# Expert routing of a two-block transformer on one NeuronCore: GpSimd's part of the look-up moved to VectorE in float16, one-hots by token pairs, expert tiles placed between the routing's parts

## The chip, the cores and the metric

The kernel runs on one core of a Trainium2 chip. The metric is the device time of one execution in microseconds (us), lower is better. The engines are named as the profile names them: PE is TensorE's matmul, PEld its weight load, DVE is VectorE, ACT is ScalarE, POOL is GpSimd, SP is SyncE, which here only issues DMAs.

## What is computed

The program is two transformer blocks over 512 tokens of width 1024 in float32. The change lies in the first block's expert layer (PEER): every token picks, in each of 8 heads, 16 of 16,384 experts by a product of two key tables of 128 keys each.

```python
def chunk(xc):                                   # 128 tokens at a time
    q = (xc @ peer_wq).reshape(TOKEN_CHUNK, PEER_HEADS, PEER_DQ)
    s1 = jnp.einsum('chd,nd->chn', q[..., :half], peer_keys[0])
    s2 = jnp.einsum('chd,nd->chn', q[..., half:], peer_keys[1])
    v1, i1 = lax.top_k(s1, PEER_TOPK)            # 16 best of 128 keys
    v2, i2 = lax.top_k(s2, PEER_TOPK)
    cand_s = (v1[..., :, None] + v2[..., None, :]).reshape(TOKEN_CHUNK, PEER_HEADS, -1)
    cand_i = (i1[..., :, None] * N_KEYS + i2[..., None, :]).reshape(TOKEN_CHUNK, PEER_HEADS, -1)
    top_s, pos = lax.top_k(cand_s, PEER_TOPK)    # 16 best of 256 pairs
    e = jnp.take_along_axis(cand_i, pos, axis=-1)
    g = jax.nn.softmax(top_s, axis=-1)
    h = jax.nn.gelu(jnp.einsum('cd,chkd->chk', xc, peer_u[e]))
    return jnp.einsum('chk,chkd->cd', g * h, peer_v[e])
```

## The kernel before

A scheduler orders each engine's instructions ahead of time from the order of the program and from its own estimate of when each can start. The order on every engine is then fixed; an instruction waits in its engine's queue until its inputs and its buffer are there, and everything behind it waits too.

The expert layer is `peer` (from L558). Three of the four blocks of 128 tokens (ND = 3, 384 tokens) are done densely: for each of the 128 expert tiles of 128 experts, TensorE computes all the products of tokens and experts, and a weight table of tokens by experts, zero where a token did not pick an expert, multiplies them. The fourth block is done by gathering the picked rows with indirect DMAs that GpSimd issues (L777 to L796). The stages are these.

1. Queries and first top-16. 16 query tiles of `peer_wq` are multiplied (L635), scored against the keys (L640), and VectorE picks 16 of 128 by its 8-wide maximum, its index search and its replacing of found values (L646 to L650).
2. Routing, the loop over the token blocks `order` = 0, 1, 3, 2 (L682 to L770). GpSimd copies the key indices to float32 (`fi`, L684) and adds the two lists to 256 sums per head (`cand`, L690); VectorE picks 16 of 256 (L696 to L700). The key index behind each pick is looked up with a one-hot over 16 places: VectorE compares (`oh`, L723, float32, four heads at a time), GpSimd multiplies by the indices (L725), VectorE adds up (`e`, L726).
3. Weight table. For the three dense blocks, VectorE makes one-hots over the 128 keys for 8 tokens at a time in float16, `o1` and `o2` (L758), and `og`, which is `o1` times the gate's high and low part (L761). The tokens lie in groups of four beside each other (`iota4`, `by4`). For each token TensorE multiplies the one-hots with a contraction over the picks (L766), ScalarE copies four tokens' results to `wb` (L768), and a DMA stores 32 tokens' table in HBM (`w_d`, L770). There are 48 such steps of 8 tokens, 96 instructions each of `o` and `og`, and 768 matmuls of 128 columns.
4. Ahead tiles. 68 of the 128 expert tiles (NA) have no need of the routing for their product of tokens and experts; `ahead` (L654) computes it (24 matmuls of 384 columns, L264 to L266), applies the gelu (L610) and stores it (`gh_d`, L656). In the program these calls stand after the routing (L822, L826); the scheduler places them on TensorE between the routing's matmuls.
5. Main loop over 32 groups of four expert tiles (L831 to L846): weights loaded from the table (L800, two buffers `wt`), `up` for the next group (L803), the split of a value tile into a high part and a rest (`v_split`, L668, two buffers each, one tile ahead), and 18 matmuls of 512 columns per tile (L844).

The expert tiles come through the class `Stream` (L221): SP loads a tile of 128x1024 (L235), ScalarE rounds it to TensorE's short float format (`wh`, L245), and GpSimd subtracts to get the rest (`wl`, L247). With `dve=0` no subtraction of this stream goes to VectorE. Raw tile, high part and rest share a pool of 12 buffers.

Of the kernel before, what the change touches and what calls it, by code (L numbers as in the profile page):

```python
# [9 lines left out]
F32R = mybir.dt.float32r  # L10
# [8 lines left out]
P = 128  # L19
# [201 lines left out]
class Stream:  # L221


    def __init__(self, c, srcs, raw=3, ahead=1, pool=None, dve=0):
        self.pool, self.dve = pool, dve
        self.c, self.srcs, self.rawn, self.ahead = c, srcs, raw, ahead
        self.raw, self.split = {}, {}
        self.i = self.nl = self.ns = 0
        self.limit = len(srcs)
# [9 lines left out]
    def do_split(self, n):  # L239
        c = self.c  # L240
        while self.ns < min(n, self.limit):
            self.load(self.ns + 1)
            r = self.raw.pop(self.ns)
            h, lo = c.t4("wh", F32R, pool=self.pool), c.t4("wl", F32R, pool=self.pool)
            c.nc.scalar.copy(h, r)  # L245
            eng = c.nc.vector if self.dve and self.ns % self.dve == 0 else c.nc.gpsimd
            eng.tensor_sub(lo, r, h)  # L247
            self.split[self.ns] = (h, lo)
            self.ns += 1
            self.load(self.ns + self.rawn - 1)  # L250
# [307 lines left out]
def peer(c, st, st_u, last):  # L558
# [56 lines left out]
    iota16 = iota[:, 0:16]  # L615

    iota4 = c.sm("iota4", [P, P, 4], F16, bufs=1)
    nc.vector.tensor_copy(iota4, iota[:, :, None].to_broadcast([P, P, 4]))
# [39 lines left out]

    esB = Pools(c)
# [8 lines left out]
    def v_split(et):  # L668

        if et >= NE:  # L670
            return
        r = vraw.pop(et)
        h, lo = (vp.tile([P, D], F32R, name=f"v{n}{et}", tag=f"v{n}", bufs=2) for n in "hl")
        for e in range(2):
            s = slice(e * 512, (e + 1) * 512)
            nc.scalar.copy(h[:, s], r[:, s])  # L676
            (nc.vector if e % 2 else nc.gpsimd).tensor_sub(lo[:, s], r[:, s], h[:, s])  # L677
        vsplit[et] = (h, lo)
        v_load(et + VRAW)


    for i in order:  # L682
        fi = se("fi", [P, 8, 2, 16], bufs=2)
        nc.gpsimd.tensor_copy(fi, ti[i])  # L684
        ts = se("ts", [P, 8, 16], bufs=2)
        px = se("px", [P, 8, 16], U32, bufs=2)
        for h4 in range(2):
            hs = slice(h4 * 4, h4 * 4 + 4)
            cand = c.t4("cand", pool=c.c4x).rearrange("p (h a b) -> p h a b", h=4, a=16)
            nc.gpsimd.tensor_tensor(cand, tv[i][:, hs, 0, :, None].to_broadcast([P, 4, 16, 16]),  # L690
# [20 lines left out]
        for half in range(2):  # L711
            pu = se("pu", [P, 8, 16], U32, bufs=2)
            if half == 0:
                nc.vector.tensor_scalar(pu, px, 4, None, op0=OP.logical_shift_right)
            else:
                nc.vector.tensor_scalar(pu, px, 15, None, op0=OP.bitwise_and)
            pf = se("pf", [P, 8, 16], bufs=2)
            nc.vector.tensor_copy(pf, pu)
            e = se("e", [P, 8, 16], bufs=4)
            for h4 in range(2):  # L720
                hs = slice(h4 * 4, h4 * 4 + 4)
                oh = c.t4("oh", pool=c.c4x).rearrange("p (h a b) -> p h a b", h=4, a=16)
                nc.vector.tensor_tensor(oh, pf[:, hs, :, None].to_broadcast([P, 4, 16, 16]),  # L723
                                        iota16[:, None, None, :].to_broadcast([P, 4, 16, 16]), op=OP.is_equal)
                nc.gpsimd.tensor_tensor(oh, oh, fi[:, hs, half, None, :].to_broadcast([P, 4, 16, 16]), op=OP.mult)  # L725
                nc.vector.tensor_reduce(e[:, hs, :], oh, axis=AX.X, op=OP.add)  # L726
            idx.append(e.rearrange("p h k -> p (h k)"))
# [10 lines left out]
        if i == order[-1]:  # L738
            esE.close()
            vp = esB.open("c8", 2)  # L740
            for et in range(VRAW):
                v_load(et)
            v_split(0)
# [6 lines left out]
        shape = [P, TG // 4, P, 4]  # L750
        by4 = lambda a: a.rearrange("p (q t) -> p q t", t=4)[:, :, None, :].to_broadcast(shape)
        for b in range(P // TB):
            wb = c.sm("wb", [P, NE, TB], bufs=2)
            for h in range(TB // TG):
                ts = slice(b * TB + h * TG, b * TB + (h + 1) * TG)
                o1, o2 = c.sm("o1", shape, F16, bufs=1), c.sm("o2", shape, F16, bufs=3)
                for o, a in ((o1, 0), (o2, 1)):
                    nc.vector.tensor_tensor(o, iota4[:, None, :, :].to_broadcast(shape), by4(sl[:, a, ts]), op=OP.is_equal)  # L758
                og = [c.sm("og", shape, F16, bufs=5) for _ in range(2)]
                for n in range(2):  # L760
                    nc.vector.tensor_mul(og[n], o1, by4(gs[:, n, ts]))  # L761
# [36 lines left out]
    def weights(gi):  # L798
        wt = c.sm("wt", [P, GE * SD], bufs=2).rearrange("p (b e t) -> p b e t", b=SD // TB, e=GE)
# [1202 lines left out]
def build(tc, ins, outs, at, phases=(1, 2, 3)):  # L2002
    nc = tc.nc
    with ExitStack() as es:
# [23 lines left out]
        if n1 + n2:  # L2028
# [13 lines left out]
            if 2 in phases:  # L2042
                peer(c, st, Stream(c, [ins["uT"][k] for k in pre_tiles()]), last)
# [32 lines left out]
```

## Time and profile before

| What | Value |
|---|---|
| median of 3 runs | 3082.31 us (3079.56 to 3094.72) |
| the profiled execution's own time | 3063.27 us |
| its span | 3061.3 us |
| mean granted clock of TensorE | 0.957 |
| PE / PEld / DVE / ACT / POOL busy | 93% / 80% / 75% / 39% / 59% |
| stretch of stages 2 to 4 in the profile | about 411 to 853 us |
| stretch of stage 5 | about 853 to 1655 us |

The durations that the profile gives come from the one profiled execution. Busy time counts the time from the start to the end of an instruction; successive instructions of one engine overlap a little, so the time from start to start is shorter than the duration. [...] For an idle time the profile names the instruction whose end released it.

### The profile page before, as it was taken

The page shows a single profiled execution, that of the slowest core. Times are in us where ns is not written, and L with a number is a line of the kernel's source. Part 1 is how long each engine was busy: PE and PEld are TensorE (multiplying, and loading weights), DVE is VectorE, ACT ScalarE, POOL GpSimd, SP SyncE. Part 2 cuts the span into 40 slices and gives each one's busy share as a digit, 9 for nine tenths or more (in the row PEclk, how much of TensorE's full clock was granted, in tenths as well). Part 3 has the DMA queues.
Part 4 walks back from the last instruction along what each step waited for, and adds up shares of the span by engine and source line. Part 5 has one row for each costly group of instructions (what it writes and reads, how often), then busy time and mean ns, then how long its engine had stood idle before and what let it go on. Part 6 is the DMA issues. An engine that isn't in the chain of part 4 may idle for free. (4 is left out here: it accounts for less than half of the span.)

```text
span 3061.3 us, 42565 instructions
## 1 busy us (share of the span) xinstructions
PE 2855.0 (93%) x15507; PEld 2433.8 (80%) x15507; DVE 2309.1 (75%) x3734; ACT 1208.4 (39%) x2077; POOL 1806.8 (59%) x1231
## 2 busy tenths in 40 slices
PE   6789997889999999999999899899999998999998
PEld 5557897779978888888887677688887877888887
DVE  7985899997188999999998688968345874477721
ACT  4444334456333333333334432211225764444431
POOL 5544465543667888888885376623347754554444
PEclk9789998999999999999999999998999999999999
DMA  3101244446799999999996555453753226322232
GB/s 131 41 14 57 77 129 127 173 156 249 237 338 316 327 335 335 323 324 341 332 336 212 177 161 165 139 172 104 222 159 99 76 70 214 120 90 93 93 96 76
DMA packets 270918, 554.01 MB, mean 181 GB/s; under 512 B 41394, under 2 KB 147890, under 8 KB 268916
## 3 DMA queue, kind: packets, MB, share of 16 engines
q1 hardware_dynamic: 219264, 370.91, 37.8%
q0 software_dynamic: 36864, 134.23, 12.0%
q10 hardware_dynamic: 14580, 46.15, 4.2%
q8 instruction: 122, 2.00, 0.3%
q14 instruction: 88, 0.72, 0.1%
HBM read 464.77 MB, written 83.89 MB: 179 GB/s over the span
## 5 line engine op out<-in xcount | busy, mean ns | idle before, releaser
L247 POOL TENSOR_TENSOR wl<-wr,wh 128x1024 fp32r<-128x1024 f32 x319 | 812.9, 2550 | 557.8 <-ACT wh L245 297.9
L245 ACT CAST wh<-wr 128x1024 fp32r<-128x1024 f32 x319 | 334.7, 1050 | 611.5 <-PE mm L265 201.3
L788 DVE CUSTOM_DVE_ANT_0 ur<-ur,hnt 128x1024 f32<-128x1024 f32 x128 | 216.8, 1695 | 74.2 <-DMA ur<-in_u,eix 72.9
L779 POOL DMA_INDIRECT ur<-in_u,eix x128 | 169.5, 1324 | 63.7 <-DVE hc L788 34.4
L677 POOL TENSOR_TENSOR vl<-vr,vh 128x512 fp32r<-128x512 f32 x128 | 190.9, 1492 | 23.6 <-ACT vh L676 18.1
L677 DVE TENSOR_TENSOR vl<-vr,vh 128x512 fp32r<-128x512 f32 x128 | 183.4, 1433 | 25.8 <-issue 16.8
L796 DVE SCALAR_TENSOR_TENSOR acc<-vr,hc,acc 128x1024 f32<-128x1024 f32 x128 | 193.5, 1512 | 1.8 <-DMA vr<-in_vrow,eix 1.7
L779 POOL DMA_INDIRECT vr<-in_vrow,eix x128 | 155.5, 1215 | 47.1 <-issue 24.0
L676 ACT CAST vh<-vr 128x512 fp32r<-128x512 f32 x256 | 145.6, 619 | 76.2 <-issue 31.1
L844 PE MATMUL pb<-vl,ah 128*128 128x512 f32 x512 | 168.9, 397 | 0.0
L844 PE MATMUL pb<-vh,al 128*128 128x512 f32 x512 | 166.4, 395 | 0.0
L844 PE MATMUL pb<-vh,ah 128*128 128x512 f32 x512 | 163.1, 399 | 2.4 <-ACT ah L817 2.4
L766 PE MATMUL pb<-og,o 128*128 128x128 f16 x768 | 105.8, 296 | 41.6 <-DVE og L761 41.2
L766 PEld LDWEIGHTS <-o 128*128 128x128 f16 x768 | 82.7, 119 | 59.6 <-DVE og L761 28.5
L768 ACT ACTIVATE wb<-pb 128x512 f32<-128x512 f32 x96 | 98.9, 1139 | 71.6 <-PE pb L766 71.1
L353 DVE SCALAR_TENSOR_TENSOR acc<-hp,vecs,acc 128x512 f32<-128x512 f32 x100 | 115.8, 1173 | 0.7
L844 PEld LDWEIGHTS pb<-vh,ah 128*128 128x128 f32 x512 | 97.3, 190 | 23.7 <-ACT ah L817 2.7
L844 PEld LDWEIGHTS pb<-vl,ah 128*128 128x128 f32 x512 | 97.2, 190 | 23.0
L844 PEld LDWEIGHTS pb<-vh,al 128*128 128x128 f32 x512 | 97.2, 190 | 22.9
L758 DVE TENSOR_TENSOR o<-iota,sl 128x1024 f16<-128x1024 f16 x96 | 105.4, 1126 | 11.1 <-ACT sl L737 6.9
L1927 POOL TENSOR_TENSOR prob<-prob,nz 128x128 f32<-128x128 f32 (+3 forms) x128 | 88.6, 724 | 39.4 <-DVE nz L1924 27.6
L1152 DVE TENSOR_TENSOR tot<-tot,sq 128x512 f32<-128x512 f32 x11 | 17.0, 1548 | 112.9 <-ACT sq L1149 112.9
(1404 smaller groups left out, 8991.0 us busy)
## 6 DMA issues: line engine op xcount, KB each, us to landing
wr<-in_ws SPq DMA_DIRECT2D x191, 512.0 KB
wr<-in_uT SPq DMA_DIRECT2D x128, 512.0 KB
vr<-in_vrow SPq DMA_DIRECT2D x128, 512.0 KB
w_d<-wb ACTq DMA_DIRECT2D x12, 2048.0 KB
wt<-w_d SPq DMA_DIRECT2D x32, 768.0 KB
gh_d<-gh ACTq DMA_DIRECT2D x68, 192.0 KB
gh<-gh_d SPq DMA_DIRECT2D x68, 192.0 KB
rd_d<-z SPq DMA_DIRECT2D x24, 256.0 KB
```

The costliest lines, as they stand in the source:

```text
L245: c.nc.scalar.copy(h, r)
L247: eng.tensor_sub(lo, r, h)
L353: nc.vector.scalar_tensor_tensor(acc[j], hp[:, tap:tap + S], w[:, tap:tap + 1], acc[j], op0=OP.mult, op1=OP.add)
L676: nc.scalar.copy(h[:, s], r[:, s])
L677: (nc.vector if e % 2 else nc.gpsimd).tensor_sub(lo[:, s], r[:, s], h[:, s])
L758: nc.vector.tensor_tensor(o, iota4[:, None, :, :].to_broadcast(shape), by4(sl[:, a, ts]), op=OP.is_equal)
L766: nc.tensor.matmul(wp[:, u * P:(u + 1) * P], o2[:, q, :, u], og[n][:, q, :, u], start=n == 0, stop=n == 1)
L768: nc.scalar.activation(wb[:, :, t4:t4 + 4].rearrange("p e t -> p t e"), wp.rearrange("p (t e) -> p t e", t=4), AF.Copy, scale=1.0 / GSCALE)
L779: nc.gpsimd.indirect_dma_start(out=t, out_offset=None, in_=src, in_offset=bass.IndirectOffsetOnAxis(ap=eix[:, s:s + 1], axis=0))
L788: nc.vector.tensor_tensor_reduce(out=u, in0=u, in1=hnt, scale=1.0, scalar=0.0, op0=OP.mult, op1=OP.add, accum_out=hc[:, s:s + 1])
L796: nc.vector.scalar_tensor_tensor(acc, v, ghs[gi][:, s:s + 1], acc, op0=OP.mult, op1=OP.add)
L844: nc.tensor.matmul(outs[i][half], ps[a][:, ts], vs[v][:, half * 512:(half + 1) * 512], start=et == 0 and n == 0, stop=et == NE - 1 and n == 2)
```

## The change

Five things are changed.

- The subtractions `wl` of 46 expert tiles (numbers 12 to 57 of this stream) go from GpSimd to VectorE (`dve=range(NTOP, NTOP + NROUTE)`).
- The routing no longer uses GpSimd: `cand` is added on VectorE, `fi` is made there in float16 with each index written twice, and the look-up runs in float16 on 2048 elements at once: one comparison with a table of places, one multiplication, three halving additions and a last one.
- The one-hots over 128 keys are laid out by pairs of tokens (`iota2`, `by2`) where they were by groups of four. The counts and sizes of the instructions stay; TensorE reads every second element where it read every fourth.
- The ahead tiles are called between the routing's parts: 12 ahead of it, 4 at the start of each token block, and one in two of three steps of 8 tokens.
- In the main loop the value tiles are split three ahead (four buffers each of high part and rest) and the weights are loaded two groups ahead (three buffers).

```diff
@@ class Stream
-            eng = c.nc.vector if self.dve and self.ns % self.dve == 0 else c.nc.gpsimd
+            eng = c.nc.vector if self.ns in self.dve else c.nc.gpsimd
             eng.tensor_sub(lo, r, h)
@@ constants
+VAHEAD = 3
 NA = 68
+NTOP = 12
+NSEL = 4
+NROUTE = NT * NSEL + ND * 10
@@ def peer
-    iota4 = c.sm("iota4", [P, P, 4], F16, bufs=1)
+    iota2 = c.sm("iota2", [P, P, 2], F16, bufs=1)
...
+    place = c.sm("place", [P, 16, 16], F16, bufs=1)
+    nc.vector.tensor_copy(place, iota[:, 0:16, None].to_broadcast([P, 16, 16]))
...
+    ahead(NTOP)
...
-        h, lo = (vp.tile([P, D], F32R, name=f"v{n}{et}", tag=f"v{n}", bufs=2) for n in "hl")
+        h, lo = (vp.tile([P, D], F32R, name=f"v{n}{et}", tag=f"v{n}", bufs=VAHEAD + 1) for n in "hl")
...
     for i in order:
-        fi = se("fi", [P, 8, 2, 16], bufs=2)
-        nc.gpsimd.tensor_copy(fi, ti[i])
+        ahead(NSEL)
+
+        fi = se("fi", [P, 2, P, 2], F16, bufs=2)
+        for half in range(2):
+            nc.vector.tensor_copy(fi[:, half].rearrange("p (h a) t -> p h a t", h=8),
+                                  ti[i][:, :, half, :, None].to_broadcast([P, 8, 16, 2]))
...
-            nc.gpsimd.tensor_tensor(cand, tv[i][:, hs, 0, :, None].to_broadcast([P, 4, 16, 16]),
+            nc.vector.tensor_tensor(cand, tv[i][:, hs, 0, :, None].to_broadcast([P, 4, 16, 16]),
...
+            oh = c.t4("oh", F16, 2048, pool=c.c4x)
+            oj = oh.rearrange("p (h j k) -> p h j k", h=8, j=16)
+            nc.vector.tensor_tensor(oj, pf[:, :, None, :].to_broadcast([P, 8, 16, 16]),
+                                    place[:, None, :, :].to_broadcast([P, 8, 16, 16]), op=OP.is_equal)
+            ok = oh.rearrange("p (j k t) -> p j k t", k=8, t=2)
+            nc.vector.tensor_mul(ok, ok, fi[:, half, :, None, :].to_broadcast([P, P, 8, 2]))
+            for n in (8, 4, 2):
+                nc.vector.tensor_add(oj[:, :, 0:n, :], oj[:, :, 0:n, :], oj[:, :, n:2 * n, :])
             e = se("e", [P, 8, 16], bufs=4)
-            for h4 in range(2):
-                hs = slice(h4 * 4, h4 * 4 + 4)
-                oh = c.t4("oh", pool=c.c4x).rearrange("p (h a b) -> p h a b", h=4, a=16)
-                nc.vector.tensor_tensor(oh, pf[:, hs, :, None].to_broadcast([P, 4, 16, 16]),
-                                        iota16[:, None, None, :].to_broadcast([P, 4, 16, 16]), op=OP.is_equal)
-                nc.gpsimd.tensor_tensor(oh, oh, fi[:, hs, half, None, :].to_broadcast([P, 4, 16, 16]), op=OP.mult)
-                nc.vector.tensor_reduce(e[:, hs, :], oh, axis=AX.X, op=OP.add)
+            nc.vector.tensor_add(e, oj[:, :, 0, :], oj[:, :, 1, :])
...
-            v_split(0)
+            for et in range(VAHEAD):
+                v_split(et)
...
-        shape = [P, TG // 4, P, 4]
+        shape = [P, TG // 2, P, 2]
...
             for h in range(TB // TG):
+                if (b * (TB // TG) + h) % 3:
+                    ahead(1)
...
-                            nc.tensor.matmul(wp[:, u * P:(u + 1) * P], o2[:, q, :, u], og[n][:, q, :, u], start=n == 0, stop=n == 1)
+                            nc.tensor.matmul(wp[:, u * P:(u + 1) * P], o2[:, q * 2 + u // 2, :, u % 2],
+                                             og[n][:, q * 2 + u // 2, :, u % 2], start=n == 0, stop=n == 1)
...
-        wt = c.sm("wt", [P, GE * SD], bufs=2).rearrange("p (b e t) -> p b e t", b=SD // TB, e=GE)
+        wt = c.sm("wt", [P, GE * SD], bufs=3).rearrange("p (b e t) -> p b e t", b=SD // TB, e=GE)
...
-            v_split(et + 1)
+            v_split(et + VAHEAD)
@@ def build
-                peer(c, st, Stream(c, [ins["uT"][k] for k in pre_tiles()]), last)
+                peer(c, st, Stream(c, [ins["uT"][k] for k in pre_tiles()], dve=range(NTOP, NTOP + NROUTE)), last)
```

In the changed kernel's line numbers L774 makes the one-hots (L758 before), L777 their products (L761 before), L683 the rests of the value tiles (L677 before), and L661, L785 and L787 are L656, L768 and L770 before. L732, L735, L737 and L739 are the new look-up. The numbers behind the names only tell buffers apart.

The first place is VectorE's queue in the routing, where one token block's look-up meets another block's one-hots. Before:

```order
L758 TENSOR_TENSOR o_746_3762<-iota_534_2466,sl_3639 128x1024
L758 TENSOR_TENSOR o_738_3731<-iota_534_2466,sl_3639 128x1024
L707 RECIPROCAL gz_4153<-gz_4153 128x8
L723 TENSOR_TENSOR oh_4162<-pf_4159,iota_2464 128x1024
L723 TENSOR_TENSOR oh_4166<-pf_4159,iota_2464 128x1024
L723 TENSOR_TENSOR oh_4175<-pf_4172,iota_2464 128x1024
L761 TENSOR_TENSOR og_3735<-o_738_3731,gs_3642 128x1024
L761 TENSOR_TENSOR og_3736<-o_738_3731,gs_3642 128x1024
L708 TENSOR_TENSOR g_4150<-g_4150,gz_4153 128x128
L758 TENSOR_TENSOR o_752_3790<-iota_534_2466,sl_3639 128x1024
L726 TENSOR_REDUCE e_4161<-oh_4162 128x64
```

The same engine and place with the change:

```order
L777 TENSOR_TENSOR og_4638<-o_884_4634,gs_4197 128x1024
L777 TENSOR_TENSOR og_4639<-o_884_4634,gs_4197 128x1024
L247 TENSOR_TENSOR wl_5101<-wr_5036,wh_5100 128x1024
L735 TENSOR_TENSOR oh_6215<-oh_6215,fi_6156 128x2048
L774 TENSOR_TENSOR o_902_4725<-iota_534_2466,sl_4194 128x1024
L735 TENSOR_TENSOR oh_6227<-oh_6227,fi_6156 128x2048
L706 MAX ts_6377<-cand_6379 128x8 x4
L774 TENSOR_TENSOR o_890_4662<-iota_534_2466,sl_4194 128x1024
L247 TENSOR_TENSOR wl_5255<-wr_5070,wh_5254 128x1024
L737 TENSOR_TENSOR oh_6215<-oh_6215 128x8x128
```

The expert tiles' subtractions (L247) now stand in VectorE's queue about every sixth row, and the multiplications of the look-up (L735) too.

The second place is GpSimd's queue in the routing. Before:

```order
L690 TENSOR_TENSOR cand_3580<-tv_2470 128x1024
L684 CAST fi_3554<-ti_2474 128x256
L684 CAST fi_4102<-ti_2475 128x256
L247 TENSOR_TENSOR wl_5489<-wr_5424,wh_5488 128x1024
L247 TENSOR_TENSOR wl_5523<-wr_5458,wh_5522 128x1024
L247 TENSOR_TENSOR wl_5557<-wr_5492,wh_5556 128x1024
L725 TENSOR_TENSOR oh_3614<-oh_3614,fi_3554 128x1024
L725 TENSOR_TENSOR oh_3618<-oh_3618,fi_3554 128x1024
```

With the change:

```order
L247 TENSOR_TENSOR wl_3908<-wr_3843,wh_3907 128x1024
L683 TENSOR_TENSOR vl_6473<-vr_6466,vh_6472 128x512
L683 TENSOR_TENSOR vl_6481<-vr_6468,vh_6480 128x512
L683 TENSOR_TENSOR vl_6489<-vr_6470,vh_6488 128x512
L683 TENSOR_TENSOR vl_7715<-vr_6478,vh_7714 128x512
L247 TENSOR_TENSOR wl_7208<-wr_7057,wh_7207 128x1024
```

The first row is the last expert tile ahead of the routing; the next is the first value tile's split, which belongs to the routing's end. Between them GpSimd has nothing in its queue.

The third place is ScalarE's queue at the last store of the weight table, in which the numbers behind `gh_d` count the ahead tiles from 0 to 67. Before:

```order
L656 DMA gh_d46_2441<-gh_1318_6912 128x384
L768 ACTIVATE wb_1053_5187<-pb_1070_5252 128x4x128
L768 ACTIVATE wb_1053_5187<-pb_1071_5262 128x4x128
L768 ACTIVATE wb_1053_5187<-pb_1076_5280 128x4x128
L768 ACTIVATE wb_1053_5187<-pb_1077_5290 128x4x128
L770 DMA w_d_2463<-wb_1053_5187 128x4096
L245 CAST wh_1340_7052<-wr_1332_6988 128x1024
```

With the change:

```order
L661 DMA gh_d58_2453<-gh_1371_7334 128x384
L785 ACTIVATE wb_1331_7115<-pb_1358_7248 128x4x128
L785 ACTIVATE wb_1331_7115<-pb_1359_7258 128x4x128
L785 ACTIVATE wb_1331_7115<-pb_1364_7276 128x4x128
L785 ACTIVATE wb_1331_7115<-pb_1365_7286 128x4x128
L245 CAST wh_1393_7474<-wr_1385_7410 128x1024
L787 DMA w_d_2463<-wb_1331_7115 128x4096
```

Before, 21 ahead tiles (47 to 67) were left when the table was done; with the change 9 are left (59 to 67).

## Rows read from the trace of the kernel before

**Rows 1.** The page, part 2: busy tenths in 40 slices of 76.5 us.
```profile
PE   6789997889999999999999899899999998999998
...
DVE  7985899997188999999998688968345874477721
...
POOL 5544465543667888888885376623347754554444
```

**Rows 2.** Stretches: from:to, length, PE PEld DVE ACT POOL (instructions), PEclk, DMA share, GB/s.
```profile
411.00:762.00 351.00, 306.80 (x1915) 288.35 (x1914) 329.53 (x550) 179.26 (x213) 196.07 (x77) 0.93 0.50 171
762.00:853.00 91.00, 88.64 (x508) 87.83 (x507) 17.09 (x23) 30.09 (x45) 53.83 (x30) 1.00 0.77 253
853.00:1655.00 802.00, 786.54 (x3703) 679.13 (x3702) 746.82 (x775) 284.56 (x526) 655.69 (x430) 0.99 0.92 325
```

**Rows 3.** Waits from 411 to 762 us: us in all, times, longest us.
```profile
POOL wl L247 <- ACT wh L245: 103.5, 23, 12.5
...
PE pb L766 <- DVE og L761: 41.2, 25, 7.6
PEld L766 <- DVE og L761: 28.5, 19, 7.9
...
ACT wh L245 <- PE po L265: 16.0, 7, 3.3
```

**Rows 4.** Instructions by line, 411 to 762 us: busy us, mean ns, idle before.
```profile
L247 POOL TENSOR_TENSOR wl<-wr,wh 128x1024 fp32r<-128x1024 f32 x48 | 130.1, 2713 | 124.6 <-ACT wh L245 103.5 <-issue 14.4 <-PE po L266 5.8
...
L758 DVE TENSOR_TENSOR o<-iota,sl 128x1024 f16<-128x1024 f16 x96 | 105.4, 1126 | 11.1 <-ACT sl L737 6.9 <-PE pb L766 3.7
...
L761 DVE TENSOR_TENSOR og<-o,gs 128x1024 f16<-128x1024 f16 x96 | 98.9, 1067 | 2.0 <-PE pb L766 1.5
...
L245 ACT CAST wh<-wr 128x1024 fp32r<-128x1024 f32 x47 | 49.5, 1053 | 30.7 <-PE po L265 16.0 <-POOL wl L247 10.8 <-DMA wr<-in_uT 1.9
L725 POOL TENSOR_TENSOR oh<-oh,fi 128x1024 f32<-128x1024 f32 x16 | 47.7, 2996 | 23.2 <-DVE oh L723 23.2
L723 DVE TENSOR_TENSOR oh<-pf,iota 128x1024 f32<-128x1024 f32 x16 | 26.3, 1687 | 0.0
...
L726 DVE TENSOR_REDUCE e<-oh 128x64 f32<-128x1024 f32 x16 | 19.2, 1208 | 2.4 <-POOL oh L725 2.4
```

**Rows 5.** VectorE in order of time: start us, duration us, instruction, count.
```profile
619.45 3.48 DVE L723 TENSOR_TENSOR oh<-pf,iota 128x1024 f32<-128x1024 f32 x3
...
622.96 8.35 DVE L758 TENSOR_TENSOR o<-iota,sl 128x1024 f16<-128x1024 f16 x3
...
657.89 1.89 DVE L758 TENSOR_TENSOR o<-iota,sl 128x1024 f16<-128x1024 f16 x3
```

**Rows 6.** GpSimd in the same stretch.
```profile
625.14 8.36 POOL L725 TENSOR_TENSOR oh<-oh,fi 128x1024 f32<-128x1024 f32 x3
```

**Rows 7.** TensorE in the same stretch; in brackets the idle time before.
```profile
628.54 0.34 PE L265 MATMUL po<-px2l,wh 128*128 128x384 f32 x1
636.46 0.40 PE L766 MATMUL pb<-og,o 128*128 128x128 f16 x2 [7.58 <-DVE og L761]
...
646.00 0.34 PE L264 MATMUL po<-px4h,wh 128*128 128x384 f32 x1
...
649.30 0.34 PE L265 MATMUL po<-px2l,wh 128*128 128x384 f32 x1
```

**Rows 8.** All instances of a line: duration ns least/median/longest, first and last start.
```profile
L758 DVE TENSOR_TENSOR o<-iota,sl x96: 673/685/2897, 453.7 to 754.8; 128x1024 f16<-128x1024 f16 x96
...
L708 DVE TENSOR_TENSOR g<-g,gz x3: 2258/2422/2483, 436.4 to 631.2; 128x128 f32<-128x128 f32 x3
```

**Rows 9.** TensorE's waits in the main loop, 853 to 1655 us.
```profile
PE po L844 <- POOL vl L677: 6.3, 5, 2.3
PE po L844 <- ACT vh L676: 5.3, 2, 2.9
```

**Rows 10.** Stretches again: 50 us in the middle of the main loop.
```profile
1100.00:1150.00 50.00, 50.00 (x241) 43.44 (x240) 48.36 (x50) 18.65 (x34) 41.97 (x29) 1.00 0.94 336
```

More of the change, by code (lines that the diff above doesn't have):

```diff
@@ L221, with __init__ @@
 class Stream:
-    def __init__(self, c, srcs, raw=3, ahead=1, pool=None, dve=0):
+    def __init__(self, c, srcs, raw=3, ahead=1, pool=None, dve=()):
         self.pool, self.dve = pool, dve
@@ L614, in peer @@
     nc.gpsimd.iota(iota, pattern=[[1, P]], base=0, channel_multiplier=0, allow_small_or_imprecise_dtypes=True)
-    iota16 = iota[:, 0:16]
-    iota4 = c.sm("iota4", [P, P, 4], F16, bufs=1)
-    nc.vector.tensor_copy(iota4, iota[:, :, None].to_broadcast([P, P, 4]))
+    iota2 = c.sm("iota2", [P, P, 2], F16, bufs=1)
+    nc.vector.tensor_copy(iota2, iota[:, :, None].to_broadcast([P, P, 2]))
+    place = c.sm("place", [P, 16, 16], F16, bufs=1)
+    nc.vector.tensor_copy(place, iota[:, 0:16, None].to_broadcast([P, 16, 16]))
     keys = se("keys", [P, 2, P], bufs=1)
@@ L716, in peer @@
                 nc.vector.tensor_scalar(pu, px, 15, None, op0=OP.bitwise_and)
-            pf = se("pf", [P, 8, 16], bufs=2)
+            pf = se("pf", [P, 8, 16], F16, bufs=2)
             nc.vector.tensor_copy(pf, pu)
-            e = se("e", [P, 8, 16], bufs=4)
-            for h4 in range(2):
-                hs = slice(h4 * 4, h4 * 4 + 4)
-                oh = c.t4("oh", pool=c.c4x).rearrange("p (h a b) -> p h a b", h=4, a=16)
-                nc.vector.tensor_tensor(oh, pf[:, hs, :, None].to_broadcast([P, 4, 16, 16]),
-                                        iota16[:, None, None, :].to_broadcast([P, 4, 16, 16]), op=OP.is_equal)
-                nc.gpsimd.tensor_tensor(oh, oh, fi[:, hs, half, None, :].to_broadcast([P, 4, 16, 16]), op=OP.mult)
-                nc.vector.tensor_reduce(e[:, hs, :], oh, axis=AX.X, op=OP.add)
+            oh = c.t4("oh", F16, 2048, pool=c.c4x)
[6 more added lines that the diff above has]
+                nc.vector.tensor_add(oj[:, :, 0:n, :], oj[:, :, 0:n, :], oj[:, :, n:2 * n, :])
+            e = se("e", [P, 8, 16], bufs=4)
+            nc.vector.tensor_add(e, oj[:, :, 0, :], oj[:, :, 1, :])
             idx.append(e.rearrange("p h k -> p (h k)"))
@@ L748, in peer @@
         nc.vector.tensor_sub(gs[:, 1], gf, gs[:, 0])
-        shape = [P, TG // 4, P, 4]
-        by4 = lambda a: a.rearrange("p (q t) -> p q t", t=4)[:, :, None, :].to_broadcast(shape)
+        shape = [P, TG // 2, P, 2]
+        by2 = lambda a: a.rearrange("p (q t) -> p q t", t=2)[:, :, None, :].to_broadcast(shape)
         for b in range(P // TB):
@@ L757, in peer @@
                 for o, a in ((o1, 0), (o2, 1)):
-                    nc.vector.tensor_tensor(o, iota4[:, None, :, :].to_broadcast(shape), by4(sl[:, a, ts]), op=OP.is_equal)
+                    nc.vector.tensor_tensor(o, iota2[:, None, :, :].to_broadcast(shape), by2(sl[:, a, ts]), op=OP.is_equal)
                 og = [c.sm("og", shape, F16, bufs=5) for _ in range(2)]
                 for n in range(2):
-                    nc.vector.tensor_mul(og[n], o1, by4(gs[:, n, ts]))
+                    nc.vector.tensor_mul(og[n], o1, by2(gs[:, n, ts]))
                 for q in range(TG // 4):
@@ L822, in peer @@
     ahead(NA - NB)
-    wt = weights(0)
+    wts = [weights(0), weights(1)]
     for e in range(GE):
-        up(0, e, wt)
+        up(0, e, wts[0])
     ahead(NB)
@@ L831, in peer @@
     for gi in range(ng):
-        if gi + 1 < ng:
-            wt = weights(gi + 1)
+        if gi + 2 < ng:
+            wts.append(weights(gi + 2))
         for e in range(GE):
@@ L836, in peer @@
             if gi + 1 < ng:
-                up(gi + 1, e, wt)
-            v_split(et + 1)
+                up(gi + 1, e, wts[gi + 1])
+            v_split(et + VAHEAD)
             vs, ps = vsplit.pop(et), acts.pop(et)
```

## Prediction, made before the changed kernel was run

> **What bounds the kernel now.** I read the page's busy tenths first. In the slices of the routing VectorE stands at 9 and 8, TensorE at 7 to 9 and GpSimd at 5 and 6 [rows 1]; the reader is to see that TensorE, the busiest engine of the whole span, is not the fullest here. So I cut the program into stretches. From 411 to 762 us (start of the routing to the last one-hots) TensorE works 306.8 of 351 us at a granted clock of 0.93, VectorE 329.5 of 351. From 762 to 853 us TensorE is full again (88.6 of 91), with 21 expert tiles left over, and from 853 to 1655 us the main loop keeps it at 786.5 of 802 [rows 2]. [...]
>
> The waits tell what TensorE lacks: 41.2 us of its idle time end with `og` (L761), VectorE's product, and 28.5 us of its weight loads too [rows 3]. VectorE hardly waits (11.1 and 2.0 us ahead of its two large groups [rows 4]), so it is simply full. Why it is full stands in its durations. Its one-hots take 1126 and 1067 ns in the mean [rows 4], but the median of the same instruction on the same shape is 685 ns, the longest 2897 [rows 8]. In time: three L758 need 8.35 us from 622.96 us on, three others 1.89 us at 657.89 us [rows 5]. In the slow case GpSimd runs three multiplications of its own, from 625.14 for 8.36 us, 2.8 us each [rows 6], and TensorE then stands 7.58 us until `og` is there [rows 7]. Another row: L708, 128 elements only, takes 2.42 us [rows 8], about one GpSimd instruction. I read this as: a two-input instruction on VectorE does not run beside GpSimd's but waits for its end. Each GpSimd instruction costs VectorE some of its length.
>
> **The change, part by part.** All sums are made against the profiled execution (3063.3 us); the median of the runs shown, 3082.3 us, is 0.6% above, and I put the difference on the median.
>
> Given back on VectorE when GpSimd is silent in the routing: L758 96 x (1126 - 685 ns) = 42.3 us; L761 96 x (1067 - 685) = 36.7 us; L723 16 x (1687 - 1130) = 8.9 us, where 1130 is the pace of the row of three in 3.48 us less its overlap [rows 5]; L708 four times about 2.2 = 8.7 us (2.42 less some 0.2, an estimate of what 128 elements need by themselves). Sum 96.6 us [rows 4, 8].
>
> Added on VectorE: no row shows a float32 subtraction of 1024 elements there; the nearest is the float32 comparison of 1024 at 1.13 us, taken for it: 46 x 1.13 = 52.0 us. Its bounds are 0.60, the pace of three one-hots in 1.89 us less their overlap [rows 5], and 2.7, GpSimd's own mean for it [rows 4]; the comparison is nearest, being float32 and on the same engine. `cand` 8 x 1.13 = 9.0. `fi` 8 x 0.60 = 4.8. Comparison and multiplication of the new look-up, 2048 elements in float16 by pairs, as two one-hots each: 16 x 1.20 = 19.2 (bounds 0.60 and 2.26 each). The 32 halving and last additions fall from 1024 to 128 elements, about 1.5 us for a set of four, 8 x 1.5 = 12. Two rests of value tiles 1.2. Sum 98.2. Removed: 16 x 1.13 + 16 x 1.21 (L726) = 37.4, the waiting part of L723 being counted above. Net +60.8. VectorE's work in the stretch goes from 329.5 to 329.5 - 96.6 + 60.8 = 294 us.
>
> TensorE's work is the same; its place changes. A tile is 24 matmuls; 19 of them lie between 646.00 and 649.30 us [rows 7], so 0.174 us each and 4.17 us for a tile. Twelve more tiles stand ahead of the last table store, 9 behind it instead of 21. TensorE has 395 - 9 x 4.17 = 358 us up to the last one-hot, VectorE 294: TensorE becomes the bound. The bounds of the subtraction change little of that: at 0.60 VectorE would have 270 us, and at 2.7 some 366, 8 over TensorE. If it never waits the loop starts at 411 + 395 = 806 us, 47 us earlier. The clock gives something more: 0.93 over 351 us is 0.07 x 351 = 24.6 us of full-speed time, if TensorE was busy all that while (nothing, if it idled); half is taken, 12 us. Against that some waits stay, since one-hots of a block still follow its selection: a quarter of the idle time, 12 us. Routing: -47.
>
> ScalarE keeps its 46 copies and its copies of results, 179 of 351 us [rows 2]. GpSimd loses its 130 + 48 us [rows 4]; I cost its emptiness at nothing. In its queue the first value tiles' rests, eleven subtractions and then the gathers of the fourth block now stand right behind the last tile ahead of the routing, so nothing of them is late.
>
> SP's queue: loads of the expert tiles now stand further ahead of the first value rows, 57 rather than 46. DMA share is 0.50 there [rows 2], so this costs nothing. The weights: three groups instead of two are read behind the last table write, and 9 tiles (37 us) cover write and read, where 21 (87 us) did. The last write of 2 MB and three loads of 0.77 MB take 4.3 MB / 253 GB/s [rows 2] = 17 us: still hidden; if not, TensorE waits the rest at the loop's start.
>
> Main loop: TensorE idles 15.5 of 802 us, and 6.3 and 5.3 us of that are waits for the value tiles' rest and high part [rows 9], which three-ahead splitting meets. The middle of the loop shows 240 matmuls in 50 us [rows 10]; 3744 matmuls at that pace are 780 us, so 22 us is the most. I take 6, since DMA is at 0.92 and VectorE at 747 of 802 [rows 2] and both will be late next. Block 2's order shifts a little: 0, plus or minus 10.
>
> Sum: -47 - 12 + 12 - 6 = **-53 us**: 3010 for the profiled execution, **3029** off the median.
>
> [...]
>
> **The rivals.**
>
> A. All goes well: clock fully regained, few waits, the loop at its steady pace: -47 - 25 + 6 - 20 = -86, 2996 us. For it: VectorE would have 60 us to spare. Against: the loop's DMA at 0.92.
>
> B. VectorE inherits GpSimd's waits. GpSimd waited 103.5 us for ScalarE's copies (L245) ahead of 48 subtractions [rows 3]; in VectorE's queue one-hots stand behind them. 46/48 of 103.5 is 99, VectorE 294 + 99 = 393, then the 37 us of tiles: 411 + 430 = 841, -12, 3070 us. Against: GpSimd waited because it was early; the fixed order sets the subtraction where its input is expected.
>
> C. Pairs don't run at the packed pace. Then 192 one-hot instructions take 1.13 instead of 0.60, +102 us, the look-up +10: VectorE 406, loop at 411 + 406 + 37 = 854, +1, 3083 us. For it: no row shows pairs. Against: groups of four run at 0.60.
>
> [...]
>
> D. Slower: a ring. ScalarE's copy waits in its queue behind results of TensorE, VectorE's subtraction waits for that copy, one-hots wait behind the subtraction, and TensorE waits for them. If copy and subtraction, 1.05 [rows 4] + 1.13 us, stand in series with TensorE for each of 46 tiles, that is 46 x 2.18 = 100: -53 + 100 = +47, 3129 us. It cancels the gain from 1.15 us for a tile, and decides for slower by 15 us from 1.5 us on. For it: ScalarE's copies already waited 16.0 us for TensorE [rows 3]. Against: 12 buffers, so that copies can run several tiles ahead.
>
> E. The slow one-hots aren't GpSimd's doing, so nothing is given back: VectorE's stretch of 351 us grows by 60.8 to 412, 411 + 412 + 37 = 860, +7, 3089 us. For it: the rows show only that both are long at the same time. Against it: three at once [rows 5, 6] and 128 elements in 2.42 us [rows 8].
>
> **How the numbers follow.** Forecast 0.63; A 0.13; B 0.07; C 0.04; E 0.03; D 0.10. 0.5%, 15 us, is about what a measurement of this kernel can tell from no change. Faster by more: forecast and A, 0.76. Within: B, C and E, 0.14. Slower: D, 0.10. The forecast's own bounds (clock 0 to 25, waits 0 to 30, loop 0 to 20, block 2 plus or minus 10) reach from about 2992 to 3060. The range 2990 to 3070 holds the forecast, nearly all of A, and B: some 0.8.
>
> **Right or wrong would show as follows.** Right: L774 and L777 at a mean near 0.69 us with hardly any of 2 us or more; GpSimd nearly idle from 460 to 740 us; TensorE's waits for `og` under 15 us and a clock near 1.0; last one-hot near 770, loop near 805 us; L732 and L735 near 1.2 us; waits for value tiles gone from the loop. Wrong: VectorE idle ahead of L247 until ScalarE's copy (B or D, by whether TensorE waits too); L774 near 1.13 (C); L774 still with long instances while GpSimd is silent (E); TensorE waiting for `wt` at the loop's start (cover too short).

## The result and the profile after

The changed kernel takes 2997.44 us (median of 4 runs, 2994.09 to 3004.71), the kernel before 3080.93 us beside it: ratio 0.9734, 95% interval [0.9706, 0.9762]. That is 83 us by the medians. The two profiled executions lie 67.7 us apart (3063.27 and 2995.58 us): the profiled one of the kernel before lies 7 us below the lowest of its four runs, so the profiles hold 68 of the 83 us. What follows is told by the profiles.

The page of the changed kernel, part 2, against [rows 1]:

```profile
PE   7789999998899999999997998999999999999998
...
DVE  7984899987689999999996598886336874575611
...
POOL 5543340003778888888883476523347745554444
```

GpSimd is empty in three slices of the routing, and TensorE stands at 9 there.

Now the stretch from 411 us to the main loop's first matmul, which is at 841.9 us before and at 781.6 us after. First the kernel before, in that new cut (columns as in [rows 2]):

```profile
411.00:842.00 431.00, 384.44 (x2362) 365.67 (x2360) 339.35 (x562) 206.09 (x250) 243.85 (x101) 0.94 0.54 184
```

The changed kernel, the same stretch and its part up to the last one-hots:

```profile
411.00:781.60 370.60, 347.62 (x2438) 332.84 (x2436) 310.98 (x648) 208.41 (x259) 70.02 (x36) 0.97 0.68 229
...
411.00:729.00 318.00, 303.05 (x2183) 288.76 (x2181) 301.45 (x633) 194.66 (x239) 44.01 (x18) 0.98 0.65 220
```

The stretch is 60.4 us shorter, and it divides in two: TensorE idles 23.0 us instead of 46.6 (23.6 less), and it is busy 347.6 us instead of 384.4 (36.8 less), with 76 matmuls more in it. From the first to the last matmul of the loop it is 810.4 us against 820.1; but those 76 matmuls, 13 us at 0.174 us, were done inside the loop before, so the loop itself gained nothing. It ends at 1592.0 us instead of 1662.0, and the 1400 us behind it differ by 2.5 us.

VectorE's groups of the changed kernel from 411 to 729 us, against [rows 4]:

```profile
L777 DVE TENSOR_TENSOR og<-o,gs 128x1024 f16<-128x1024 f16 x96 | 69.6, 761 | 0.8 <-PE pb L782 0.4
L774 DVE TENSOR_TENSOR o<-iota,sl 128x1024 f16<-128x1024 f16 x96 | 68.6, 738 | 3.6 <-ACT sl L750 2.1 <-PE pb L782 1.0
L247 DVE TENSOR_TENSOR wl<-wr,wh 128x1024 fp32r<-128x1024 f32 x46 | 55.8, 1214 | 9.1 <-ACT wh L245 8.9
...
L732 DVE TENSOR_TENSOR oh<-pf,place 128x2048 f16<-128x2048 f16 x8 | 9.4, 1215 | 0.0
```

And the waits there, against [rows 3]:

```profile
PE pb L782 <- DVE og L777: 11.6, 8, 3.3
...
DVE wl L247 <- ACT wh L245: 8.9, 7, 3.3
```

The one-hots are down from 1126 and 1067 ns to 738 and 761, TensorE waits 11.6 us for them instead of 41.2, and VectorE waits only 8.9 us for ScalarE's copies where GpSimd had waited 103.5.

Of the 23.0 us that TensorE still idles, 8.0 us are a single wait, at the loop's first matmul, a place that cost 2.4 us before:

```profile
PE po L861 <- ACT ah L834: 8.0, 1, 8.0
```

The copy `ah` needs the product of an expert tile's result with the weights (L832). VectorE's fixed order puts that product behind its work on the first gathered rows of the fourth block (L805). GpSimd begins the first gather at 765.1 us, right behind its subtraction for an ahead tile; VectorE starts on the first row at 770.9 us after 41.5 us idle, and L832 begins at 780.0 us with no idle time ahead of it. In the 8.4 us after the loop's start the granted clock, which the profile gives as a share of TensorE's full speed, is 0.64.

### The profile page after: what moved, and what is told of

Its sections match the earlier page's. It is cut to its first block, busy times and chain, and to the rows that moved or that the text cites. A ratio compares the mean times of both kernels' runs of the same rounds, so it can differ in the third digit from the quotient of the medians.

```text
span 2993.8 us, 42580 instructions
## 1 busy us (share of the span) xinstructions
PE 2812.0 (94%) x15507; PEld 2395.3 (80%) x15507; DVE 2242.7 (75%) x3813; ACT 1203.3 (40%) x2077; POOL 1644.9 (55%) x1157
## 5 line engine op out<-in xcount | busy, mean ns | idle before, releaser
L247 POOL TENSOR_TENSOR wl<-wr,wh 128x1024 fp32r<-128x1024 f32 x273 | 695.6, 2550 | 538.0 <-ACT wh L245 254.0
L683 POOL TENSOR_TENSOR vl<-vr,vh 128x512 fp32r<-128x512 f32 x128 | 200.9, 1575 | 244.9 <-ACT vh L682 243.5
L805 DVE CUSTOM_DVE_ANT_0 ur<-ur,hnt 128x1024 f32<-128x1024 f32 x128 | 231.5, 1809 | 44.0 <-DMA ur<-in_u,eix 42.8
L813 DVE SCALAR_TENSOR_TENSOR acc<-vr,hc,acc 128x1024 f32<-128x1024 f32 x128 | 232.5, 1816 | 0.2
L796 POOL DMA_INDIRECT ur<-in_u,eix x128 | 176.6, 1379 | 42.2 <-issue 16.3
L683 DVE TENSOR_TENSOR vl<-vr,vh 128x512 fp32r<-128x512 f32 x128 | 143.7, 1129 | 27.3 <-issue 14.4
L785 ACT ACTIVATE wb<-pb 128x512 f32<-128x512 f32 x96 | 98.2, 1151 | 34.4 <-PE pb L782 33.4
L861 PE MATMUL po<-vl,ah 128*128 128x512 f32 x256 | 86.5, 402 | 12.2 <-POOL vl L683 8.1
L861 PE MATMUL po<-vh,ah 128*128 128x512 f32 x256 | 85.1, 399 | 12.4 <-ACT ah L834 12.4
L861 PE MATMUL po<-vh,al 128*128 128x512 f32 x256 | 86.3, 402 | 0.0
```

Of the source, the lines that this page charges most:

```text
L796: nc.gpsimd.indirect_dma_start(out=t, out_offset=None, in_=src, in_offset=bass.IndirectOffsetOnAxis(ap=eix[:, s:s + 1], axis=0))
L805: nc.vector.tensor_tensor_reduce(out=u, in0=u, in1=hnt, scale=1.0, scalar=0.0, op0=OP.mult, op1=OP.add, accum_out=hc[:, s:s + 1])
L813: nc.vector.scalar_tensor_tensor(acc, v, ghs[gi][:, s:s + 1], acc, op0=OP.mult, op1=OP.add)
L861: nc.tensor.matmul(outs[i][half], ps[a][:, ts], vs[v][:, half * 512:(half + 1) * 512], start=et == 0 and n == 0, stop=et == NE - 1 and n == 2)
```

## The experiments

Loop start and end are the first and last matmul of the main loop in each run's trace; the ratio is to the kernel before on the same chip. The medians are of 4 to 12 runs, in e4 and e11 of two; the loop's start and end come from one profiled execution each.

| Run | median us | ratio [95%] | table matmul, median ns | loop start, end us |
|---|---|---|---|---|
| before | 3080.93 | 1 | 297 | 841.9, 1662.0 |
| changed | 2997.44 | 0.9734 [0.9706, 0.9762] | 218 | 781.6, 1592.0 |
| e1 changed, fours | 3017.07 | 0.9788 [0.9742, 0.9835] | 297 | 808.7, 1615.5 |
| e2 before, pairs | 3067.02 | 0.9959 [0.9929, 0.9989] | 218 | 833.8, 1656.1 |
| e3 changed, singles | 3073.02 | 0.9962 [0.9934, 0.9990] | 219 | 860.0, 1658.3 |
| e4 changed, eights | 3140.31 | 1.0181 [1.0117, 1.0244] | 413 | 930.5, 1738.7 |
| e5 subtractions on GpSimd | 3041.71 | 0.9867 [0.9845, 0.9890] | 218 | 822.2, 1629.2 |
| e6 look-up on GpSimd | 3020.77 | 0.9800 [0.9776, 0.9823] | 218 | 803.8, 1607.4 |
| e7 no placement | 2990.16 | 0.9713 [0.9682, 0.9744] | 218 | 760.0, 1584.8 |
| e8 depth of before | 3009.67 | 0.9775 [0.9751, 0.9800] | 218 | 779.5, 1593.7 |
| e9 before, GpSimd's part moved | 3117.24 | 1.0136 [1.0078, 1.0193] | 297 | 790.0, 1704.0 |
| e10 = e9 and pairs | 3088.28 | 1.0033 [1.0004, 1.0061] | 219 | 761.3, 1671.5 |
| e11 = e5 in halves | 3031.26 | 0.9843 [0.9800, 0.9886] | 218 | 814.4, 1621.3 |
| e12 = e7, ten more tiles | 3004.74 | 0.9757 [0.9724, 0.9790] | 219 | 756.0, 1609.3 |

### The step at which TensorE reads: e1 to e4

The trace of the changed kernel had a surprise, 61.0 us busy in the table's 768 matmuls where the kernel before has 105.8. Only the layout of their operands differs. Four kernels vary it.

e1, the changed kernel with G = 4 in place of 2 (e3 and e4: G = 1 and 8):

```diff
-    iota2 = c.sm("iota2", [P, P, 2], F16, bufs=1)
+    iota2 = c.sm("iota2", [P, P, G], F16, bufs=1)
...
-        shape = [P, TG // 2, P, 2]
+        shape = [P, TG // G, P, G]
...
-    nc.tensor.matmul(wp[...], o2[:, q * 2 + u // 2, :, u % 2], og[n][:, q * 2 + u // 2, :, u % 2], ...)
+    nc.tensor.matmul(wp[...], o2[:, (q * 4 + u) // G, :, (q * 4 + u) % G], og[n][:, (q * 4 + u) // G, :, (q * 4 + u) % G], ...)
```

> The changed kernel with the one-hots in groups of four again (TensorE reads every fourth element), all else as changed. Theory P (the step at which TensorE reads sets the pace of the table's matmuls, and TensorE is the bound of the routing): the 768 matmuls go from 61 us busy (224 ns) back to about 106 us (296 ns); VectorE's one-hots stay at 683 ns; the main loop starts 35 to 45 us later than the changed kernel's 781.6 us, total about 3030 to 3042 us. Rival V (only VectorE's freedom from GpSimd counts): matmuls may be slower, but the loop's start moves by less than 8 us and the total stays within 10 us of 2997.

e2, the kernel before with the same edit of its `iota4`, G = 2.

> The kernel before with nothing changed but pairs for groups of four. Theory P + VectorE is the bound there: table matmuls fall from 106 to about 61 us busy, TensorE's waits for og grow from 41 us to 70 to 85, total 0 to 15 us below 3081. Rival (TensorE's work is the bound before, too): total 40 to 45 us below.

> The changed kernel with the one-hots token by token: TensorE reads neighbouring elements, VectorE's second operand then is one value repeated. [...]

> The changed kernel with groups of eight: TensorE reads every eighth element (16 bytes). If its pace falls in proportion to the step beyond pairs: table matmuls take 180 us or more, total 3100 us and above. If it is a fixed price for any step above 4 bytes: about 106 us as with fours, total that of the run with fours within 10 us.

TensorE's order of time holds runs of these matmuls behind each other (start us, us from the first's start to the last's end, count). The changed kernel, step of 2 elements:

```profile
627.99 1.90 PE L782 MATMUL pb<-og,o 128*128 128x128 f16 x30
```

e3, neighbouring elements:

```profile
623.18 0.96 PE L782 MATMUL pb<-og,o 128*128 128x128 f16 x14
```

e1, a step of 4:

```profile
623.71 3.70 PE L782 MATMUL pb<-og,o 128*128 128x128 f16 x30
```

e4, a step of 8:

```profile
628.71 3.46 PE L782 MATMUL pb<-og,o 128*128 128x128 f16 x14
```

With the last one's own duration (0.22, 0.22, 0.30 and 0.41 us) taken off, one follows another by 0.74 / 13 = 0.057 us at step 1, 1.68 / 29 = 0.058 at step 2, 3.40 / 29 = 0.117 at step 4 and 3.05 / 13 = 0.235 at step 8. The granted clock is 1.00 in the changed kernel's stretch, and runs of matmuls of 384 columns next to them follow one another by 0.17 to 0.18 us in all four, so the clock is not what makes the difference. In these four runs a step of two float16 elements (4 bytes) costs nothing, and beyond that the time grows in proportion. Theory P holds: 768 x (0.117 - 0.058) = 45 us, and the group's busy time fell by 44.8. Which of the two operands causes it was not tried; both have the step.

What the pace is worth depends on the bound. In the changed kernel fours move the loop's end by 23.5 us: TensorE is busy 36.5 us more from 411 us to the loop and idles 9.4 us less. e1's stretch, against the changed kernel's:

```profile
411.00:808.70 397.70, 384.13 (x2438) 369.79 (x2436) 312.01 (x648) 211.65 (x258) 71.56 (x37) 0.99 0.63 215
```

In the kernel before, pairs move the loop's end by 5.9 us only: TensorE is busy 29.7 us less and idles 21.6 us more, since VectorE was the bound there, busy 329.5 of 351 us [rows 2]. So e1's 35 to 45 us were too many (the loop starts 27.1 us later, and 3017 us lies under the 3030 to 3042 expected): I had counted no idle time that more work could fill. Rival V, under 8 us, is out. In e2 TensorE's waits for `og` came to 62 us where 70 to 85 were expected, and the total to 18 us less where 15 were the most. e4 came as expected, with 3140 us. e3 took 3073 us; its table matmuls have a median of 219 ns, for 218 in the changed kernel, and the granted clock from 411 us to its loop is 0.88.

e3 shows VectorE's side. With one token a row the one-hots take 1217 ns in the median, with pairs 683, with fours 684, with eights 690: in these runs two neighbours are enough for VectorE, and a step of two elements costs TensorE nothing (0.058 us for 0.057). Of the four layouts tried, pairs are the only one good for both. This is also the answer on rival C, which had pairs at 1.13 us in place of 0.60: they take 683 ns, as fours do, and only single tokens take 1217.

### GpSimd beside VectorE: e5, e6 and e11

```diff
-  peer(c, st, Stream(..., dve=range(NTOP, NTOP + NROUTE)), last)
+  peer(c, st, Stream(..., dve=()), last)
```

> The changed kernel with the 46 subtractions back on GpSimd, all else as changed. Theory G (a GpSimd instruction holds VectorE's two-input instructions up): one-hots' means go from 738 and 761 ns to 950 or more, VectorE gets back 56 us of subtractions and loses 70 to 100 in waiting, the loop starts 10 to 35 us later than 781.6, total 3008 to 3032 us. Rival (only GpSimd's queue order mattered, or nothing here): means stay under 800 ns, total within 8 us of 2997, or under it since VectorE has less to do.

e6 puts the lines of the old look-up back (`cand`, `fi`, the multiplication on GpSimd, float32).

> The changed kernel with the look-up of before (float32, GpSimd's 8 additions, 4 casts and 16 multiplications of 3 us), all else as changed. Theory G: GpSimd's 68 us of instructions hold VectorE up for 30 to 50 us, one-hots' means 850 to 950 ns, total 3005 to 3035 us. Rival (the look-up cost little: its instructions were few): total within 8 us of 2997.

e11 is e5 with each of the 46 subtractions cut in two:

```diff
-            eng.tensor_sub(lo, r, h)
+            parts = 2 if self.ns in self.dve else 1
+            for e in range(parts):
+                s = slice(e * (P * 8 // parts), (e + 1) * (P * 8 // parts))
+                c.nc.gpsimd.tensor_sub(lo[:, s], r[:, s], h[:, s])
```

> The changed kernel with the 46 subtractions on GpSimd, as in e5, but each as two of 512 columns. Theory L (VectorE waits until the GpSimd instruction that is running ends): the longest one-hots fall from 2.9 us to 2.1 us or less, their count of long ones grows, the means stay within 100 ns of e5's 976 and 1037. [...]

With the subtractions back on GpSimd the one-hots take 976 and 1037 ns, and the loop ends 37.2 us later; the median is 44 us above the changed kernel, 10 more than I had allowed, and the loop starts 40.6 us later where 35 was the most. The rival is out: VectorE has 46 instructions less and is slower. With the look-up back they take 791 and 884 ns, where 850 to 950 were expected, and the loop ends 15.4 us later; the total, 3021 us, is in the range expected.

How the one holds up the other shows in order of time. e5, VectorE and then GpSimd:

```profile
621.59 3.48 DVE L777 TENSOR_TENSOR og<-o,gs 128x1024 f16<-128x1024 f16 x2
```

```profile
621.47 2.44 POOL L247 TENSOR_TENSOR wl<-wr,wh 128x1024 fp32r<-128x1024 f32 x1 [6.26 <-ACT wh L245]
```

GpSimd ends at 623.91; two one-hots at their pace of 0.6 us from there end at 625.1, and VectorE's pair ends at 621.59 + 3.48 = 625.07. Nothing of the first was done before GpSimd's end. e11, the same with halves:

```profile
624.17 1.66 DVE L776 TENSOR_TENSOR o<-iota,sl 128x1024 f16<-128x1024 f16 x1
625.87 2.27 DVE L779 TENSOR_TENSOR og<-o,gs 128x1024 f16<-128x1024 f16 x2
```

```profile
623.41 3.58 POOL L249 TENSOR_TENSOR wl<-wr,wh 128x512 fp32r<-128x512 f32 x2 [4.88 <-ACT wh L245]
```

One one-hot of 1.66 us ends at 625.83, the next pair at 628.14: VectorE slips in between the halves, which lie from 623.41 to 626.99. So it waits for the end of the one instruction (theory L), and shorter ones make shorter waits, but as many more: the means stay at 974 and 1019 ns, as expected. Up to 732 us, while GpSimd has halves only, none of e11's one-hots takes more than 1.79 us and 49 of 167 take over 1 us; in e5 up to there the longest takes 2.90 us and 26 of 159 take over 1 us. That the two only slow each other down side by side is out by that. That the longest of all would fall under 2.1 us was wrong, because 14 other subtractions of this stretch are still whole; the longest one-hots left (2885 and 2894 ns) are of their length, as 741.59 us, where a pair of 3.38 us stands beside a whole one of 2.50.

### Placement and depth: e7, e8, e9, e10 and e12

```diff
-    ahead(NTOP)
...
-        ahead(NSEL)
...
-                if (b * (TB // TG) + h) % 3:
-                    ahead(1)
```

> The changed kernel with all ahead tiles called after the routing again, as before the change. Theory T (TensorE is the bound and needs tiles at hand while one-hots are late): more tiles stand behind the last table store and TensorE's idle time between 411 us and the loop grows from 23 to 40 us or more, total 3010 to 3035 us. Rival (the scheduler finds the places by itself): order nearly the same, total within 8 us of 2997.

e8: `VAHEAD = 1`, `wt` with two buffers, `weights(gi + 1)` one group ahead.

> The changed kernel with value tiles split one ahead (two buffers each) and weights loaded one group ahead (two buffers), as before. Theory D (the depth does nothing: the loop's waits for value tiles are 12.1 us in the changed kernel and 15.1 before): total within 8 us of 2997, loop within 5 us of its 810. Rival (the depth is what took the 10 us from the loop): loop 818 to 822 us, total 3005 to 3012 us; slower still if TensorE waits for the weights at the loop's start.

e9: in the kernel before, `dve=range(12, 58)` and the new look-up, nothing else; e10: pairs besides.

> The kernel before with only GpSimd's part of the routing moved: the 46 subtractions and the look-up on VectorE; groups of four, no placement, depth of before. If the parts add up as the runs so far say by the loop's end (pairs 23, subtractions 37, look-up 15, placement -7, depth 2 us): 52 us before the 1662 us of the kernel before, so about 1610, total 3010 to 3025 us. Rival (parts lean on each other, the move is worth little without pairs): loop's end above 1630, total above 3035 us.

> The run with only GpSimd's part moved, and pairs besides; no placement, depth of before. By the same sums the loop ends 75 us earlier than before, at about 1587, total 2983 to 3000 us: as fast as the changed kernel or up to 0.5% faster, which says that placement and depth are worth nothing. Rival (the three-ahead depth is worth the 12 us that the medians of the run without it show): 3000 to 3012 us.

e12: e7 with `dve=range(NTOP, NA)`.

> The changed kernel without placement (e7, 2990 us) and with the subtractions of the last ten ahead tiles on VectorE too. GpSimd's 8 to 11 subtractions between 650 and 760 us hold one-hots up there; VectorE has room (41 of 50 us busy). Theory G: one-hots' means fall from 770 and 726 to about 700 ns, the loop ends 0 to 8 us before e7's 1585, total 2980 to 2990 us. Rival (TensorE is the bound there, or the loads of the tiles): total within 5 us of 2990.

e7 fell on its rival's side: the scheduler finds places by itself. The loop starts earlier and ends 7 us earlier, and the interval overlaps the changed kernel's, so I call it equal. e8 is open: in its trace the loop ends only 1.7 us later, but that execution (2997 us) is the fastest of its five, the other four take 3008 to 3016, and the median, 12 us above the changed kernel's, is what the rival forecast; the intervals overlap. Then e9 and e10, without both, missed by about 100 us: they reach the loop 52 and 81 us earlier than the kernel before and then need 914 and 910 us for it. e10 is e7 without the depth, and e8 without the placement, so it is their absence together that costs. The two parts of the depth, value tiles and weights, were not tried apart. Against the kernel before, e10's loop idles 60.3 us more, and is busy 29.8 us longer with the same 3791 matmuls, at a granted clock of 0.97 instead of 0.99.

Where the time goes in the loop of e10: first a stretch, then ScalarE's waits from 900 to 1100 us.

```profile
860.00:1660.00 800.00, 727.74 (x3304) 616.52 (x3304) 620.93 (x691) 253.70 (x471) 559.38 (x385) 0.97 0.84 290
```

```profile
ACT ah L823 <- PE pb L850: 88.3, 23, 9.2
```

And TensorE's in e10 from 790 to 1680 us:

```profile
PE po L850 <- POOL vl L678: 36.0, 21, 4.4
PE po L850 <- DVE vl L678: 30.6, 17, 4.4
```

No engine is full: TensorE 728 of 800, VectorE 621, DMA 0.84. In e7 the same line `ah` waits for no matmul:

```profile
ACT ah L829 <- DVE mm L827: 43.1, 12, 6.4
```

A likely cause shows in the fixed order. Between the value tile's copy `vh` and the products' copies `ah`, both in ScalarE's queue, this is how many `ah` more than the tile's number stand ahead of `vh`:

| value tile | 16 | 24 | 32 | 40 | 48 | 56 | 72 | 96 | 104 |
|---|---|---|---|---|---|---|---|---|---|
| before | 3 | 3 | 3 | 3 | 3 | 3 | 3 | 3 | 3 |
| changed | 3 | 2 | 2 | 2 | 2 | 2 | 2 | 3 | 3 |
| e7 | 2 | 2 | 2 | 2 | 2 | 2 | 2 | 3 | 3 |
| e9, e10 | 7 | 7 | 8 | 7 | 6 | 3 | 3 | 3 | 3 |
| e8 | 6 | 6 | 3 | 3 | 3 | 3 | 3 | 3 | 3 |
| e12 | 3 | 2 | 3 | 3 | 3 | 6 | 8 | 7 | 6 |

In e9 and e10 the copies `ah` of a later group stand ahead of the value tile that TensorE needs now. `ah` waits for a buffer that TensorE's product `pb` frees, the value tile's `vh` waits behind it, `vl` waits for `vh`, and TensorE waits for `vl`: a ring, as I read it. e12 is an instance of its own, at other tiles and another time; its one-hots are close to their pace without GpSimd (687 and 698 ns, as expected) and yet it takes 3005 us, above what it and its rival expected, and its loop ends 24.5 us later than e7's. ScalarE's wait and the stretch from 1200 to 1300 us of e12:

```profile
ACT ah L829 <- PE pb L856: 33.5, 9, 6.5
```

```profile
1200.00:1300.00 100.00, 83.02 (x383) 70.02 (x381) 78.75 (x94) 30.05 (x56) 77.72 (x51) 0.98 0.90 319
```

From 900 to 1200 us, before that wait appears, its TensorE works 97.6 to 99.7 of every 100 us. In e9, e10 and e12 the wait of `ah` for `pb` appears with the large lead; in the kernel before, in e7 and, up to 1500 us, in the changed kernel it is absent. e8 has a lead of 6 or 7 at tiles 12 to 28 only, and 5.2 us of that wait; the changed kernel has a lead of 6 at tiles 108 to 120, and 3.7 us of it. This is a correlation in seven traces, not a test: no kernel was run with that order alone mended. Open is also the later part of e10, 1200 to 1500 us, where TensorE works 87 to 93 of 100 us without that wait.

## Why the prediction was right, and where it was not

The direction, the range and the cause in the first place held: 2997 lies in 2990 to 3070, near its lower end, and by the profiles the gain is 67.7 us where 53 was forecast. But some 19 of the 67.7 us come from something that the sum put at nothing, the layout's price on TensorE. With that undone, in e1, the profiles lie 48.3 us apart (the medians 68, on their own chip). Of the terms:

- **VectorE freed of GpSimd**: right. In e5 and e11 VectorE's one-hots, which read two tiles, wait for GpSimd's end (623.91 us in e5, the pair behind it done at 625.07), and e6's means of 791 and 884 ns agree. The forecast had the one-hots at 685 ns; the means are 738 and 761, because 14 subtractions stayed on GpSimd in this stretch (e12, with ten more on VectorE, has 687 and 698). VectorE's work came to 301 us up to 729 us; forecast 294.
- **The price of a subtraction on VectorE**: forecast 1.13 us, measured 1.214, so 46 of them took 55.8 us for 52.0. Of the new look-up's two large instructions, forecast at 1.20 each, the comparison took 1.215 and the multiplication 1.463.
- **"TensorE's work is the same; its place changes"**: wrong, and the step that failed. The pair layout took 44.8 us off the table's matmuls. The prediction weighed pairs for VectorE only (rival C) and left the operand's step at TensorE out of the sum. e1 is the kernel that the sum described, with a table matmul's median at 297 ns, as before. Its loop ends 46.5 us earlier than in the kernel before, where 47 was forecast for the routing and 6 for the loop. The changed kernel's ends 70.0 us earlier, so the step is worth 23.5 us.
- **TensorE's waits**: the term -47 + 12 = -35, the 46.6 us that [rows 2] leave idle from 411 to 853 us (442 less 306.8 and 88.6) and a quarter of them kept, came to -32.9 in e1, with 13.6 us idle, 1.4 of them for `og`. In the changed kernel it came to -23.6: TensorE, done sooner with each matmul, waits 11.6 us for `og` again. In both, the first gathers, of which the prediction said that nothing is late, hold up the loop's start, by 8.9 and 8.0 us.
- **The clock**: forecast 12 us. In e1 TensorE is busy as long as before (384.1 and 384.4 us) with 76 matmuls more, 13 us at 0.174 us, and the granted clock is 0.99 instead of 0.94: some 13 us. In the changed kernel, of the 36.8 us less busy time, 44.8 is the layout and 13 the other way the further matmuls, which leaves some 5 for the clock, at 0.97. So waits and clock were nearly right for the kernel that the sum described. That the time with the faster matmuls is still in the range, 7 us above its lower end, is luck: no bound of it was meant for them.
- **Placement**: forecast as the means by which TensorE gets its tiles. e7 shows that the scheduler does as well without the calls.
- **The loop**: forecast -6 by depth; the loop's own gain is nothing. TensorE still waited 8.1 us for `vl` in it. That depth and placement together keep the loop from costing 90 us more was not in the forecast at all.
- **Rivals**: A gave 2996, nearly the measured time, but by a loop at its steady pace and a full clock, and neither came; B and D are out, with 8.9 us of waits of VectorE for ScalarE's copies; C is out by 683 ns and E by e5. A ring is what e9, e10 and e12 suggest, though in the main loop and through other instructions than rival D's.
- **The bounds**: added up, the bounds of the forecast's terms reach from 2980 to 3075 us, not from 2992 to 3060.
- **Handing work away from a full VectorE**: in e5, with the subtractions handed to GpSimd, the loop ends 37.2 us later.

## What to carry to other kernels

Work that VectorE and GpSimd divide should be priced with the wait: in e5 a GpSimd subtraction of 2.44 us stretched a pair of one-hots from 1.29 to 3.48 us, so a slower-looking engine assignment can free more than it adds; here 46 subtractions added 55.8 us to VectorE, and the loop starts 40.6 us earlier than in e5. The layout of a tile had a price on writer and reader (VectorE 1217 ns at singles for 683 at pairs, TensorE 0.117 us at fours for 0.058); look at both before choosing a step, here two float16 elements for both. And where a scheduler fixes the order, a gain upstream can be paid back further down, as in e9 and e10, which reach the loop 52 and 81 us earlier and leave it 42 and 9.5 us later: compare the whole span, and the end of the next stage, not the start.

## What was not expected of the hardware

TensorE's matmul of 128 columns of float16 follows the one before it by 0.057 and 0.058 us with operands at steps of 2 and 4 bytes, 0.117 us at 8 bytes and 0.235 us at 16. VectorE's float16 comparison of 1024 elements took 683 to 690 ns with inner runs of 2, 4 or 8 and 1217 ns without one.
